# A transformer-layer kernel: ten adding DMAs sent at other weight units, cross-output differences kept in PSUM, two row turns moved together, one weight split put later

## The chip, the cores and the metric

The kernel runs on one core of one Trainium2 chip. The metric is the device time of one execution in microseconds (us). TensorE multiplies matrices (PE in the profile, its weight loads PEld), VectorE (DVE) and ScalarE (ACT) do elementwise work, GpSimd (POOL) does small elementwise work and issues DMAs of its own, and SyncE (SP) issues most of the weight loads.

## The reference

One layer of a bidirectional encoder on 512 tokens of width 1024, in float32. It has three sub-layers, and each is added to the residual after a norm:

```python
h = rmsnorm(x, pre_mix_g)                                  # 1. token mixing
aq, ak, av, hq, hf_fwd, hf_bwd, hi, hg = split_columns(h @ w_in, IN_SPLITS)
att = axial_gqa_attention(rope(norm(aq)), rope(norm(ak)), av)
rec = hgrn2_group(hq, hf_fwd, hf_bwd, hi, hg, lb, hg_out_norm_g)
x = x + rmsnorm(concat([att, rec]) @ w_out, post_mix_g)
h = rmsnorm(x, pre_x_g); m = rmsnorm(mem, mem_norm_g)      # 2. cross-attention, 256 memory rows
x = x + rmsnorm(memory_cross_attention(h, m, w_xq, w_xkv, w_xo), post_x_g)
h = rmsnorm(x, pre_ffn_g)                                  # 3. gated MLP
u = depthwise_conv3(h @ w_up) + conv_b                     # 2 x 2816 columns
gate, val = split(u, 2)
x = x + rmsnorm((silu(gate) * val) @ w_down, post_ffn_g)
```

## The kernel before

**Products.** Every large product is made of three matmuls on float32r halves: an operand is split into a high part (a cast, on ScalarE) and a low part (the difference, on VectorE), and `mm3` (lines 323 to 325) adds high times high, high times low and low times high in a PSUM bank. PSUM has eight banks of 128 x 512, two for each of the four tags "b", "s", "c" and "o"; a new tile of a tag waits until the oldest of its two is released by its last reader.

**Weight units.** Weights come in units of 128 x 1024 (512 KB). SP loads a unit into a `raw` buffer (line 229; two of them), `issue` casts it to `wh` on ScalarE (line 267) and subtracts to `wl` on VectorE (line 269). For some units the low part is made otherwise: ScalarE or GpSimd writes -wh (lines 274, 272) and a DMA of GpSimd's queue adds the weights to it in flight (line 275). A unit is issued three ahead of its use. Units 38 to 45 are the mixing output projection, 46 to 49 the memory values, 50 to 57 the queries, 58 to 71 the cross output, and from 72 (`N_UP`) on the up-projection.

**Weight sums.** The down-projection uses sums of weight blocks (the Strassen-Winograd scheme: seven products in place of eight). They are made in DRAM by DMAs alone: a *seed* copies a first block to `sum_t` (line 293, SP's queue, after units 28 to 45 and 60 to 65), and later an *add* adds the second block to it in flight (line 296, GpSimd's queue). There are 24 adds, in a fixed order; the set `adds_at` names the units after which one goes out. Ten of its entries are `ADDS_AT`, the others are units of the up-projection. GpSimd first copies one column of the unit's `wl` to `mark` (line 281), so that the add follows that unit's low part. Every sixth add is half as large.

**Mixing output and queries.** `res_second` takes units 42 to 45 for the second half of the output columns, row block by row block. For each block of 128 rows the output is squared and summed on ScalarE (line 377), GpSimd makes the inverse root (lines 348, 351), VectorE multiplies by the gain (379) and adds to x (384), ScalarE squares again (401), VectorE scales (355), TensorE turns the rows (line 362), and ScalarE and VectorE split the turned rows (151, 152). The queries (units 50 to 57) then multiply them; `put_qx` splits each product (lines 1094, 1095). Meanwhile SP loads the eight half blocks of the cross output weights (line 1106) and VectorE adds them in place (line 1111).

**Cross output.** The output of the cross-attention is again seven products in place of eight, with running sums in PSUM: `near_y` (tag "c"), `far_y` ("s") and `last_y` ("b"). Four small steps take a difference or a sum with a kept product: `far_near` (line 1205), `far_far` (1210), `near_far` (1215) and `near_done` (1228); each writes a tile in SBUF, which the norm of that half row block then squares and multiplies. Row blocks 2 and 3 ("far") are turned while the last products run (`OUT_TURN`). Row blocks 0 and 1 ("near") are turned in the up-projection.

**Start of the up-projection.** Its first four products (`us`, banks b, s, c, o) run first on the far 256 columns, then on the near 256. `UP_TURN` names the product n of the first part after which a near row block is turned: (1, 2) turns block 0 after product 1 and block 1 after product 2.

**What sets the order.** The order of instructions on each engine is fixed when the program is built, by a scheduler that follows the order of the code and its own estimate of times. `tc.issue_after(ins)` puts the block's instructions behind `ins` on the engine of `ins`.

Of the kernel before, what the change touches and what calls it, by code (L numbers as in the profile page):

```python
# [28 lines left out]
UP_S = (6, 8, 9, 11, 12, 14, 15, 17, 18, 20)  # L29
N_PLAIN, N_MIX, N_WHOLE = 58, 66, 110 - 2 * len(UP_S)  # L30
N_UP = N_PLAIN + 14
# [11 lines left out]
SIDES_AT = (19, 20)  # L43
LOW_FROM = {"diag": 0, "last": 512}
SEEDS_AT = frozenset(range(28, 46)) | frozenset(range(60, 66))
ADDS_AT = frozenset(range(45, 65, 2))
XO_LOADS = {1: [('w11', 0), ('w11', 1)], 2: [('w12', 0), ('w12', 1)], 3: [('w22', 0), ('w22', 1)], 4: [('w21', 0), ('w21', 1)]}
XO_AT = {"w11": 58, "w21": 60, "w12": 62, "w22": 64}
XO_FROM = {"t1": "w11", "t3": "w12", "t4": "w21", "t2": "w22"}
# [5 lines left out]
NEG_GROUP = frozenset((p, 1) for p in (2, 5, 6))  # L55
AHEAD = 3
HOLD_BLOCK = 4
TURN_STEP, MEM_TURN, UP_TURN = 0, (0, 4), (1, 2)
NEG_SCALAR = frozenset(range(9, 33))
NEG_POOL = frozenset(range(33, 42))  # L60
CORE_SHARE, ATT_LEAD = 53.0, 4.0
# [58 lines left out]
def layer(tc, io, out):  # L120
    nc = tc.nc
# [16 lines left out]
    def bank(tag):  # L138
        return ps.tile([P, 512], F32, name="ps_" + tag, tag=tag)
# [4 lines left out]
    def tmp2(shape=(P, 512), dt=F32, tag="ta"):  # L144
        return t2.tile(list(shape), dt, name="tmp2", tag=tag, bufs=TMP_BUFS[tag])

    def tmp4(shape, dt=F32):
        return t4.tile(shape, dt, name="tmp4", tag="tmp4")

    def split(hi, lo, src, eng=None):  # L150
        nc.scalar.copy(hi, src)  # L151
        (eng or nc.vector).tensor_sub(lo, src, hi.bitcast(F32))  # L152

    def split_scaled(hi, lo, src, factor):
# [22 lines left out]
    for i, name in enumerate(XO_UNITS):  # L177
# [4 lines left out]
            plan.append(("w", XO_AT[name] + u) if name in XO_AT else ("xs", (name, u)))  # L182
        if name in XO_BY_DMA:
            by_adding.add(N_PLAIN + i)
    whole, adds_at = N_MIX, set(ADDS_AT)
    for i in range(NF):
        if i in UP_S:
            plan += [(kind, UP_S.index(i)) for kind in ("diag", "side", "sums", "last")]
        else:
            if i >= 2:  # L190
                adds_at.update((len(plan), len(plan) + (i - 1 not in UP_S)))
            plan += [("w", whole), ("w", whole + 1)]
            whole += 2
    assert len(plan) == N_DOWN and whole == N_WHOLE
# [50 lines left out]
    def issue():  # L245
        i = issued[0]
        issued[0] += 1
        raw = raws.popleft() if raws else load_w()
        kind = plan[i][0] if i < N_DOWN else "w"
        if kind == "diag" and not raws:  # L250
            raws.append(load_w())
        if kind in ("side", "sums", "last"):
            raw = pair_sums[kind]
        elif kind == "xs":
            name, u = plan[i][1]
            raw = cross_blocks[XO_FROM[name]][:, u, :]
        if kind == "keep":
            kept = big([P, 2, 1024], F32R)
            wh, wl = kept[:, 0], kept[:, 1]
        else:  # L260
            wh = wp.tile([P, 1024], F32R, name="wh", tag="wh")
            wl = wp.tile([P, 1024], F32R, name="wl", tag="wl")
        if raw.shape[1] < 1024:
            wh, wl = wh[:, :raw.shape[1]], wl[:, :raw.shape[1]]
        next_to = kind == "diag" and plan[i - 4][0] == "diag"
        by_dma = 1024 if next_to else 0 if i in by_adding or i in NEG_POOL else LOW_FROM.get(kind, raw.shape[1])
        nc.scalar.copy(wh, raw)  # L267
        if by_dma:
            last_low[0] = nc.vector.tensor_sub(wl[:, :by_dma], raw[:, :by_dma], wh[:, :by_dma].bitcast(F32)).ins  # L269
        if by_dma < raw.shape[1]:  # L270
            if i in NEG_POOL:
                nc.gpsimd.tensor_scalar(wl, wh.bitcast(F32), -1.0, 0.0, op0=ALU.mult, op1=ALU.add)
            else:
                nc.scalar.mul(wl[:, by_dma:], wh[:, by_dma:].bitcast(F32), -1.0)  # L274
            nc.gpsimd.dma_start(wl[:, by_dma:], source(i)[:, by_dma:], accum_op=ALU.add)  # L275
        add_blocks(kind, raw, raws[0] if raws else None)
        pending.append((wh, wl))
        if i in SEEDS_AT:
            seeds.popleft()()
        if i in adds_at and adds:  # L280
            with tc.issue_after(nc.gpsimd.tensor_copy(mark, wl[:, 0:1].bitcast(F32)).ins):
                adds.popleft()()

    seeds, adds = deque(), deque()

# [916 lines left out]
    c21 = [tmp2(tag="tq") for _ in range(2)]  # L1202

    def far_near(b):
        nc.vector.tensor_sub(c21[b], c21[b], far_y[b])
        got[2 + b] = first_part(2 + b, c21[b])

    def far_far(b):
        c22 = tmp2(tag="tq")
        nc.vector.tensor_sub(c22, far_y[b], kept[:, 2 + b])  # L1210
        turns.append(second_part(2 + b, got[2 + b], c22))

    def near_far(b):
        c12 = tmp2(tag="tq")
        nc.vector.tensor_sub(c12, far_y[b], kept[:, b])
        got[b] = first_part(b, c12, 1)

    drain(cross_product(near_y, "a22", 1, unit(2), False, True, True, lambda b: nc.scalar.copy(c21[b], near_y[b])))
    drain(cross_product(far_y, "r2", 1, unit(2), False, True, False, far_near))
# [4 lines left out]
    far_done = last_mm[0]  # L1224
    hi, lo = left["a12"]
    def near_done(b):
        c11 = tmp2(tag="tq")
        nc.vector.tensor_add(c11, last_y[b], kept[:, b])
        return second_part(b, got[b], c11, 0, True)

    for b in range(2):
        for i in range(2):
# [76 lines left out]
    for part in range(2):  # L1309
        cols = half_t[1 - part]  # L1310
        for n in range(4):
            for kc in range(8):
                mm3(us[n][:, cols], (ws[n][0][:, kc, :], ws[n][1][:, kc, :]), hT.get(kc, cols), kc == 0, kc == 7)
            if part:
                conv(*first[n], us[n])
            elif n in UP_TURN:
                turns.popleft()()
    fulls = [big([P, 4, T]) for _ in range(2)]
    wide = [big([P, 2, 4, 256]) for _ in range(2)]
    s1, s2, s3, s4 = wide[0][:, 0], wide[0][:, 1], wide[1][:, 0], wide[1][:, 1]  # L1320
# [243 lines left out]
```

## Time and profile before

| | before |
|---|---|
| median of 3 runs | 813.32 us (813.09 to 813.73) |
| the profiled execution | 813.2 us, span 811.4 us |
| TensorE busy | 794.7 us (98%) |
| VectorE, ScalarE, GpSimd busy | 615.1, 515.7, 155.3 us |
| SP's queue (q1), GpSimd's queue (q0) | 36.0% and 29.3% of 16 DMA engines' span |
| weight loads `raw<-in_w_dram` on SP | 75, median 4.4 us from issue to landing |
| adds `sum_t<-in_wd_dram`, `sum_t<-sum_t` on GpSimd | 10 and 10 of 512 KB, median 7.9 and 8.6 us |

The span is the time from the first to the last instruction in the profile; the execution's own time is 1.8 us more. A row of the timeline has its start in us from the span's start, its length, engine, line, operation, the tile it writes and those it reads, and in brackets how long the engine had been idle and what ended the wait. A row of a windows view has, for each engine, the busy time in a stretch and the number of instructions, then the granted clock, the busy share of the DMA engines and GB/s. A row of waits has who waited for whom, the total in us, how many times, and the longest.

### The profile page before, as it was taken

The numbers are of one execution on the slowest core, as the hardware profiler recorded it, in microseconds if no ns is written. First come the engines' busy times: TensorE is split into PE (matmuls) and PEld (weight loads), VectorE is DVE, ScalarE is ACT, GpSimd is POOL, SyncE is SP. The second block draws the span as 40 slices with busy tenths as digits, with TensorE's granted clock in tenths as the row PEclk, the third lists the DMA queues.
The fourth block names the chain that finished last, engine by engine and source line by source line (L and its number), as shares of the span: only waits on it lengthen the run. The fifth ranks groups of instructions, "written<-read, shape, count | busy, mean of one in ns | idle before, by whom it ended". The sixth has DMA issues, their size and how long they took to land.

```text
span 811.4 us, 12058 instructions
## 1 busy us (share of the span) xinstructions
PE 794.7 (98%) x4474; PEld 687.2 (85%) x4474; DVE 615.1 (76%) x945; ACT 515.7 (64%) x860; POOL 155.3 (19%) x221
## 2 busy tenths in 40 slices
PE   9999999999999999999999999999999999999996
PEld 7888888899988888877888898899999999888884
DVE  5466586698796865748478859877897897998775
ACT  6675774678988864544676845556665664767651
POOL 0111201324223102401001621210210121010301
PEclk9999999999999999999999999999999999999998
DMA  8597666669878754497934839663764666378842
GB/s 302 193 265 169 134 151 131 143 178 275 225 180 197 188 197 120 113 257 265 287 64 134 212 105 255 143 157 96 202 163 121 169 168 170 100 234 285 240 116 103
DMA packets 44476, 146.19 MB, mean 180 GB/s; under 512 B 5505, under 2 KB 6785, under 8 KB 44417
## 3 DMA queue, kind: packets, MB, share of 16 engines
q1 hardware_dynamic: 29808, 100.58, 36.0%
q0 software_dynamic: 13312, 41.95, 29.3%
q10 hardware_dynamic: 1296, 2.89, 0.9%
q8 instruction: 35, 0.57, 0.3%
q14 instruction: 25, 0.20, 0.1%
HBM read 141.73 MB, written 25.17 MB: 206 GB/s over the span
## 4 chain that ended last, share of the span: by engine, by line
PE 81%; DVE 6%; ACT 5%; DMA 4%; POOL 2%; issue 2%; SPq 0%; DVEq 0%; POOLq 0%; ACTq 0%
PE ps_b L324 8%; PE ps_b L323 8%; PE ps_b L325 8%; PE ps_s L323 6%; PE ps_s L325 6%; PE ps_s L324 6%; PE ps_o L323 5%; PE ps_o L324 5%; PE ps_o L325 5%; PE ps_c L323 4%; PE ps_c L325 4%; PE ps_c L324 4%; DMA raw<-in_w_dram 4%; PE ps_c L726 2%; PE ps_o L989 2%
## 5 line engine op out<-in xcount | busy, mean ns | idle before, releaser
L267 ACT CAST wh<-raw 128x1024 fp32r<-128x1024 f32 x104 | 107.5, 1036 | 79.2 <-PE ps_b L324 21.2
L323 PE MATMUL ps_b<-big,wh 128*128 128x512 f32 (+1 forms) x364 | 129.2, 355 | 1.2 <-ACT big L151 1.1
L324 PE MATMUL ps_b<-big,wh 128*128 128x512 f32 (+1 forms) x364 | 127.5, 350 | 1.3 <-DVE big L152 1.3
L325 PE MATMUL ps_b<-big,wl 128*128 128x512 f32 (+1 forms) x364 | 127.2, 349 | 0.0
L269 DVE TENSOR_TENSOR wl<-raw,wh 128x1024 fp32r<-128x1024 f32 (+1 forms) x61 | 70.1, 1154 | 37.0 <-ACT wh L267 36.9
L323 PEld LDWEIGHTS ps_b<-big,wh 128*128 128x128 f32 x364 | 68.9, 189 | 10.6 <-ACT big L151 2.0
L324 PEld LDWEIGHTS ps_b<-big,wh 128*128 128x128 f32 x364 | 68.9, 189 | 10.1 <-DVE big L152 1.8
L325 PEld LDWEIGHTS ps_b<-big,wl 128*128 128x128 f32 x364 | 68.8, 189 | 9.0
L275 POOL DMA_DIRECT2D wl<-in_w_dram x39 | 35.1, 901 | 126.6 <-ACT wl L274 109.0
L323 PE MATMUL ps_s<-wh,big 128*128 128x512 f32 (+1 forms) x148 | 56.8, 385 | 0.1
L324 PE MATMUL ps_s<-wl,big 128*128 128x512 f32 (+1 forms) x148 | 56.2, 380 | 0.0
L325 PE MATMUL ps_s<-wh,big 128*128 128x512 f32 (+1 forms) x148 | 56.1, 379 | 0.0
L755 DVE TENSOR_TENSOR big<-big 128x512 f32<-128x512 f32 x64 | 47.6, 760 | 8.4 <-PE ps_c L726 3.5
L323 PE MATMUL ps_s<-big,wh 128*128 128x256 f32 (+1 forms) x160 | 47.9, 299 | 0.0
L325 PE MATMUL ps_s<-big,wl 128*128 128x256 f32 (+1 forms) x160 | 47.8, 299 | 0.0
L324 PE MATMUL ps_s<-big,wh 128*128 128x256 f32 (+1 forms) x160 | 47.8, 299 | 0.0
L274 ACT ACTIVATE wl<-wh 128x1024 fp32r<-128x1024 f32 (+1 forms) x46 | 44.3, 962 | 0.6
L152 DVE TENSOR_TENSOR big<-ps_o,big 128x512 fp32r<-128x512 f32 (+1 forms) x55 | 36.3, 666 | 9.0 <-ACT big L151 7.0
L267 ACT CAST wh<-big 128x1024 fp32r<-128x1024 f32 (+1 forms) x28 | 28.2, 1008 | 19.4 <-PE ps_c L325 5.6
L275 POOL DMA_DIRECT2D wl<-in_wu_dram x16 | 13.9, 869 | 133.7 <-ACT tmp L1360 120.1
L269 DVE TENSOR_TENSOR wl<-big,wh 128x1024 fp32r<-128x1024 f32 (+1 forms) x28 | 32.3, 1162 | 9.3 <-ACT wh L267 7.5
L348 POOL TENSOR_SCALAR small<-small 128x1 f32<-128x1 f32 x40 | 18.9, 473 | 87.7 <-ACT tmp L1396 40.4
(342 smaller groups left out, 2271.3 us busy)
## 6 DMA issues: line engine op xcount, KB each, us to landing
raw<-in_w_dram SPq DMA_DIRECT2D x75, 512.0 KB, 4.4
wl<-in_w_dram POOLq DMA_DIRECT2D x39, 512.0 KB, 6.5
sum_t<-in_wd_dram SPq DMA_DIRECT2D x20, 512.0 KB, 6.9
tmp<-in_w_dram SPq DMA_DIRECT2D x12, 512.0 KB, 4.9
raw<-in_wu_dram SPq DMA_DIRECT2D x12, 512.0 KB, 4.1
sum_t<-in_wd_dram POOLq DMA_DIRECT2D x10, 512.0 KB, 7.9
sum_t<-sum_t POOLq DMA_DIRECT2D x10, 512.0 KB, 8.6
big<-sum_t SPq DMA_DIRECT2D x10, 512.0 KB, 4.4
```

Source lines behind the costliest of these rows:

```text
L152: (eng or nc.vector).tensor_sub(lo, src, hi.bitcast(F32))
L267: nc.scalar.copy(wh, raw)
L269: last_low[0] = nc.vector.tensor_sub(wl[:, :by_dma], raw[:, :by_dma], wh[:, :by_dma].bitcast(F32)).ins
L274: nc.scalar.mul(wl[:, by_dma:], wh[:, by_dma:].bitcast(F32), -1.0)
L275: nc.gpsimd.dma_start(wl[:, by_dma:], source(i)[:, by_dma:], accum_op=ALU.add)
L323: nc.tensor.matmul(o, a[0], b[0], start=start, stop=False, skip_group_check=again)
L324: nc.tensor.matmul(o, a[0], b[1], start=False, stop=False, skip_group_check=again)
L325: last_mm[0] = nc.tensor.matmul(o, a[1], b[0], start=False, stop=stop, skip_group_check=again).ins
L348: nc.gpsimd.tensor_scalar(ss[:, i + 4:i + 5], ss[:, i:i + 1], 1.0 / D, ss[:, i + 3:i + 4] if i else EPS, op0=ALU.mult, op1=ALU.add)
L726: nc.tensor.matmul(o[:, b, :], kc[:, blk(b)], qc[:, blk(b)] if m == 1 else pat(qk, b * P, [[2 * m, P // (2 * m)], [T + m, 2], [1, m]]), st ...
L755: nc.vector.tensor_tensor(out=c, in0=c, in1=pat(tt, toff + off, [[2, npair], [gap, 2], [0, m]]), op=ALU.mult)
L989: nc.tensor.matmul(o, vv[:, c, h // 4].rearrange("p a d -> p (a d)"), pt[j][:, c, :], start=c + j == 0, stop=c == 3 and j == 1)
```

## The change

The ten entries of `ADDS_AT` become units 42, 43, 44 (twice), 45 (twice), 59, 60, 61 and 63, in place of 45, 47, ... 63; `adds_at` is a list now, and a unit sends as many adds as it stands there. `far_near` writes into `near_y`, `far_far` into a bank of tag "o", `near_far` and `near_done` in place, all in PSUM. `UP_TURN` becomes (2, 2): both near row blocks are turned after product 2. The cast of unit `N_UP` + 3 (75) is put on ScalarE behind the last cast that `split` has made by then, that of the last turned far rows.

```diff
--- before.py
+++ after.py
@@ -43,7 +43,7 @@
 SIDES_AT = (19, 20)
 LOW_FROM = {"diag": 0, "last": 512}
 SEEDS_AT = frozenset(range(28, 46)) | frozenset(range(60, 66))
-ADDS_AT = frozenset(range(45, 65, 2))
+ADDS_AT = (42, 43, 44, 44, 45, 45, 59, 60, 61, 63)
 XO_LOADS = {1: [('w11', 0), ('w11', 1)], 2: [('w12', 0), ('w12', 1)], 3: [('w22', 0), ('w22', 1)], 4: [('w21', 0), ('w21', 1)]}
 XO_AT = {"w11": 58, "w21": 60, "w12": 62, "w22": 64}
 XO_FROM = {"t1": "w11", "t3": "w12", "t4": "w21", "t2": "w22"}
@@ -55,7 +55,7 @@
 NEG_GROUP = frozenset((p, 1) for p in (2, 5, 6))
 AHEAD = 3
 HOLD_BLOCK = 4
-TURN_STEP, MEM_TURN, UP_TURN = 0, (0, 4), (1, 2)
+TURN_STEP, MEM_TURN, UP_TURN = 0, (0, 4), (2, 2)
 NEG_SCALAR = frozenset(range(9, 33))
 NEG_POOL = frozenset(range(33, 42))
 CORE_SHARE, ATT_LEAD = 53.0, 4.0
@@ -147,8 +147,10 @@
     def tmp4(shape, dt=F32):
         return t4.tile(shape, dt, name="tmp4", tag="tmp4")
 
+    last_high = [None]
+
     def split(hi, lo, src, eng=None):
-        nc.scalar.copy(hi, src)
+        last_high[0] = nc.scalar.copy(hi, src).ins
         (eng or nc.vector).tensor_sub(lo, src, hi.bitcast(F32))
 
     def split_scaled(hi, lo, src, factor):
@@ -182,13 +184,13 @@
             plan.append(("w", XO_AT[name] + u) if name in XO_AT else ("xs", (name, u)))
         if name in XO_BY_DMA:
             by_adding.add(N_PLAIN + i)
-    whole, adds_at = N_MIX, set(ADDS_AT)
+    whole, adds_at = N_MIX, list(ADDS_AT)
     for i in range(NF):
         if i in UP_S:
             plan += [(kind, UP_S.index(i)) for kind in ("diag", "side", "sums", "last")]
         else:
             if i >= 2:
-                adds_at.update((len(plan), len(plan) + (i - 1 not in UP_S)))
+                adds_at += sorted({len(plan), len(plan) + (i - 1 not in UP_S)})
             plan += [("w", whole), ("w", whole + 1)]
             whole += 2
     assert len(plan) == N_DOWN and whole == N_WHOLE
@@ -264,7 +266,11 @@
             wh, wl = wh[:, :raw.shape[1]], wl[:, :raw.shape[1]]
         next_to = kind == "diag" and plan[i - 4][0] == "diag"
         by_dma = 1024 if next_to else 0 if i in by_adding or i in NEG_POOL else LOW_FROM.get(kind, raw.shape[1])
-        nc.scalar.copy(wh, raw)
+        if i == N_UP + 3:
+            with tc.issue_after(last_high[0]):
+                nc.scalar.copy(wh, raw)
+        else:
+            nc.scalar.copy(wh, raw)
         if by_dma:
             last_low[0] = nc.vector.tensor_sub(wl[:, :by_dma], raw[:, :by_dma], wh[:, :by_dma].bitcast(F32)).ins
         if by_dma < raw.shape[1]:
@@ -279,7 +285,8 @@
             seeds.popleft()()
         if i in adds_at and adds:
             with tc.issue_after(nc.gpsimd.tensor_copy(mark, wl[:, 0:1].bitcast(F32)).ins):
-                adds.popleft()()
+                for _ in range(min(len(adds), adds_at.count(i))):
+                    adds.popleft()()
 
     seeds, adds = deque(), deque()
 
@@ -1202,18 +1209,17 @@
     c21 = [tmp2(tag="tq") for _ in range(2)]
 
     def far_near(b):
-        nc.vector.tensor_sub(c21[b], c21[b], far_y[b])
-        got[2 + b] = first_part(2 + b, c21[b])
+        nc.vector.tensor_sub(near_y[b], c21[b], far_y[b])
+        got[2 + b] = first_part(2 + b, near_y[b])
 
     def far_far(b):
-        c22 = tmp2(tag="tq")
+        c22 = bank("o")
         nc.vector.tensor_sub(c22, far_y[b], kept[:, 2 + b])
         turns.append(second_part(2 + b, got[2 + b], c22))
 
     def near_far(b):
-        c12 = tmp2(tag="tq")
-        nc.vector.tensor_sub(c12, far_y[b], kept[:, b])
-        got[b] = first_part(b, c12, 1)
+        nc.vector.tensor_sub(far_y[b], far_y[b], kept[:, b])
+        got[b] = first_part(b, far_y[b], 1)
 
     drain(cross_product(near_y, "a22", 1, unit(2), False, True, True, lambda b: nc.scalar.copy(c21[b], near_y[b])))
     drain(cross_product(far_y, "r2", 1, unit(2), False, True, False, far_near))
@@ -1224,9 +1230,8 @@
     far_done = last_mm[0]
     hi, lo = left["a12"]
     def near_done(b):
-        c11 = tmp2(tag="tq")
-        nc.vector.tensor_add(c11, last_y[b], kept[:, b])
-        return second_part(b, got[b], c11, 0, True)
+        nc.vector.tensor_add(last_y[b], last_y[b], kept[:, b])
+        return second_part(b, got[b], last_y[b], 0, True)
 
     for b in range(2):
         for i in range(2):
@@ -1313,8 +1318,9 @@
                 mm3(us[n][:, cols], (ws[n][0][:, kc, :], ws[n][1][:, kc, :]), hT.get(kc, cols), kc == 0, kc == 7)
             if part:
                 conv(*first[n], us[n])
-            elif n in UP_TURN:
-                turns.popleft()()
+            else:
+                for _ in range(UP_TURN.count(n)):
+                    turns.popleft()()
     fulls = [big([P, 4, T]) for _ in range(2)]
     wide = [big([P, 2, 4, 256]) for _ in range(2)]
     s1, s2, s3, s4 = wide[0][:, 0], wide[0][:, 1], wide[1][:, 0], wide[1][:, 1]
```

## The prediction

> **What bounds the kernel now.** I read the page's first lines, then the waits of TensorE, then the windows, and only then the timeline around each wait.
>
> ```profile
> span 811.4 us, 12058 instructions
> PE 794.7 (98%) x4474; PEld 687.2 (85%) x4474; DVE 615.1 (76%) x945; ACT 515.7 (64%) x860; POOL 155.3 (19%) x221
> PE ps_s L325 <- DVE big L1095: 1.6, 1, 1.6
> PE ps_b L362 <- DVE tmp L355: 1.4, 1, 1.4
> PE ps_b L324 <- DVE big L152: 1.3, 2, 0.9
> 296.00:308.00 12.00, 12.00 (x60) 9.66 (x59) 5.28 (x10) 6.08 (x11) 1.10 (x2) 1.00 0.95 335
> 345.00:385.00 40.00, 37.06 (x188) 30.88 (x186) 26.83 (x32) 17.47 (x29) 5.20 (x9) 1.00 0.85 261
> 440.00:475.00 35.00, 32.51 (x193) 27.71 (x192) 27.62 (x41) 24.47 (x50) 17.93 (x28) 1.00 0.66 166
> ```
>
> TensorE is busy for 98% of the span, and the change leaves its matmuls as they are. So only its idle time can be won, 16.7 us in all. The waits and windows say where: 2.9 us in 345 to 385 (query projection) and 2.5 us in 440 to 475 (cross output and start of the up-projection). The granted clock is 1.00 in each window, so the throttle plays no part. The profiled execution took 813.2 us, 1.8 over its span; the median of the runs, 813.3, is 0.1 above it. I sum against 813.2.
>
> **Part 1: six adding transfers leave the query stage.** Before, the adds go out after units 45, 47, ... 63; unit 45 is the last of the output projection, 46 to 49 are the memory values, 50 to 57 the queries. After, the first six go out at 42, 43, 44, 44, 45, 45 and four at 59, 60, 61, 63.
>
> ```profile
> raw<-in_w_dram SPq DMA_DIRECT2D x1, 512.0 KB, 3.3
> raw<-in_w_dram SPq DMA_DIRECT2D x1, 512.0 KB, 6.1
> q0 software_dynamic: 135, 0.49, 47.6%
> q1 hardware_dynamic: 187, 0.70, 41.2%
> 345.36 0.39 PE L324 MATMUL ps_s<-wl,big 128*128 128x512 f32 x1
> 345.59 0.39 PE L325 MATMUL ps_s<-wh,big 128*128 128x512 f32 x1
> 344.86 1.05 ACT L267 CAST wh<-raw 128x1024 fp32r<-128x1024 f32 x1 [5.20 <-DMA raw<-in_w_dram]
> 345.82 0.58 ACT L151 CAST big<-ps_c 128x512 fp32r<-128x512 f32 x1
> 348.16 0.40 PE L325 MATMUL ps_b<-big,wl 128*128 128x512 f32 x1
> ```
>
> The first two rows are weight loads on SP's queue: the one issued at 331.3 landed in 3.3 us, with no add about; the one issued at 338.64, with the add of unit 47 (issued 336.11) in flight, took 6.1. The queue rows are those of 338.6 to 344.8: q0, POOL's, held 47.6% of 6.2 us of the 16 engines, 2.95 us, nearly all of one add. So an add costs a load beside it about 2.9 us. That load was unit 50's. ScalarE stood 5.20 us at its cast, with the two casts of the last turned rows queued behind it (345.82), and TensorE needed those. Three matmul steps, 345.59 to 348.16, took 2.57 us in place of three times 0.23: **gap A, 1.9 us**. Without the adds of 47 and 49 the load lands at 341.9, the casts end at 344.0, their differences at 345.5, before TensorE asks at 345.8. I take all 1.9 (between 1.0 and 1.9).
>
> ```profile
> 380.44 0.39 PE L325 MATMUL ps_s<-big 128*128 128x256 f32 x1 [1.59 <-DVE big L1095]
> 378.56 1.22 DVE L1111 TENSOR_TENSOR big<-big 128x1024 f32<-128x1024 f32 x1
> 379.70 0.68 DVE L1095 SCALAR_TENSOR_TENSOR big<-ps_b,big 128x512 fp32r<-128x512 f32 x1
> raw<-in_w_dram SPq DMA_DIRECT2D x1, 512.0 KB, 11.8
> sum_t<-in_wd_dram POOLq DMA_DIRECT2D x1, 512.0 KB, 9.9
> ```
>
> **Gap B**, 1.6 us: the fourth query's low part, L1095, stood on VectorE behind a block sum, L1111. VectorE had a backlog because loads issued at 357 took 11.8 us beside an add of 9.9. Three adds (51, 53, 55) go from this stretch, some 2.9 us each, so loads come more than 4 us sooner while TensorE comes 1.9 sooner. The order of VectorE's queue may still put an L1111 ahead; the cast that L1095 waits for follows TensorE itself, so 0.3 or so stays. I take 1.3, all but about a fifth (0 to 1.6). Sum of part 1: -3.2.
>
> **Part 2: what the same adds cost where they go.**
>
> ```profile
> 303.93 0.33 SPq L229 DMA_DIRECT2D raw<-in_w_dram  x1
> raw<-in_w_dram SPq DMA_DIRECT2D x1, 512.0 KB, 5.5
> 311.59 1.06 ACT L267 CAST wh<-raw 128x1024 fp32r<-128x1024 f32 x1
> 312.68 1.23 DVE L269 TENSOR_TENSOR wl<-raw,wh 128x1024 fp32r<-128x1024 f32 x1 [0.35 <-ACT wh L267]
> 313.96 0.19 PEld L324 LDWEIGHTS ps_s<-wl,big 128*128 128x128 f32 x1 [0.38 <-DVE wl L269]
> raw<-in_w_dram SPq DMA_DIRECT2D x1, 512.0 KB, 3.2
> sum_t<-in_wd_dram POOLq DMA_DIRECT2D x1, 512.0 KB, 8.1
> q0 software_dynamic: 198, 0.75, 68.6%
> q1 hardware_dynamic: 194, 0.73, 34.6%
> ```
>
> Unit 45's load, issued at 303.93, stands in SP's queue behind the four rows of x and lands at 309.4. Its cast follows at 311.59, and TensorE already waits 0.38 us for its low part: 2.2 us of slack, then every us counts. DMA is 0.95 busy from 296 to 308 (row above). The add of unit 43 displaces 2.95 us there, less 0.6 idle: landing 311.7, a stall of 0.2. The two adds of unit 44 follow its difference at about 304.2 and 305. Where both queues are full they alternate (387 to 393, last two rows: 198 against 194 packets) and the adds get two thirds of the time. If they start at once after the gains, the load crawls at a third of the rate to about 316.7, a stall of 5.2. Against that, unit 46's load (313.93) had an add issued 0.3 us after it and still landed in 3.2 (the pair 3.2 and 8.1). That is the nearest row in order of issue, though without a queue ahead. So 0.2 to 5.2, taken nearer the low end: **+1.9**. A stall here shifts everything after it; nothing later gives it back.
>
> [...]
>
> POOL itself: a mark copy and a DMA issue of 0.8 to 0.9 us each. Behind 42 and 43 stand the two gains (297.93), behind 44's two the first row sums (310.50); behind 45's two, which end near 315.9, one at 316.31. None is passed. At 59 to 63 the transfers run where no weight load is due (none is issued from 391 to 419): 0, bounds -0.3 and +0.5. SP issues what it did.
>
> **Part 3: cross output, turns and the split of unit 75.**
>
> ```profile
> 459.01 1.05 ACT L267 CAST wh<-raw 128x1024 fp32r<-128x1024 f32 x1
> 461.77 0.68 DVE L152 TENSOR_TENSOR big<-ps_o,big 128x512 fp32r<-128x512 f32 x1
> 462.37 0.68 DVE L379 TENSOR_TENSOR tmp<-tmp,big 128x512 f32<-128x512 f32 x1
> 461.91 0.39 PE L324 MATMUL ps_b<-big,wh 128*128 128x256 f32 x1 [0.45 <-DVE big L152]
> 463.74 0.92 POOL L275 DMA_DIRECT2D wl<-in_w_dram  x1
> 469.15 0.66 PE L362 MATMUL ps_b<-ident,tmp 128*128 128x128 f32 x4 [1.35 <-DVE tmp L355]
> 473.18 0.62 PE L362 MATMUL ps_c<-ident,tmp 128*128 128x128 f32 x4
> 474.16 0.36 PE L323 MATMUL ps_o<-big,wh 128*128 128x256 f32 x1
> ```
>
> The cast of unit 75 (459.01) ran between the casts of the last far rows and cost ScalarE 0.95 us there; it now follows them. But VectorE does its four L152 back to back until 462.4, so the up-projection, which waits for their low parts, gains nothing from that alone. And there is a new wait: the first up product takes a bank "b", and both are last_y's. Before, L1228 freed one at 459.4; now last_y itself is squared and multiplied, so it is free after L379, at 462.4 to 463.05. The first product starts 0.6 to 1.2 us later than at 461.8.
>
> The turn of row 0 no longer stops TensorE at 467.6 (1.5 us until 469.15): three products of 2.88 run first, to about 471.3, and row 0 is ready by then. The two turns take 2.0 and end near 473.3 in place of 474.16: **-0.85**, if row 1 is ready by 472.3. It was ready at 473.1, with POOL's issue for unit 75 (463.74) just ahead of its row sum; unit 75's moved chain and ScalarE's 0.95 should give that 0.6 to 0.8. Bounds: -1.8 (row 1 early, bank free early) and +0.7 (row 1 no earlier, bank late). Unit 75's low part landed at 469.1 and is used at 474: 5 us of cover; moved by 2 us it costs nothing, moved by more than 5 each us counts. The differences written to PSUM are the same VectorE instructions, 0.68 us; the multiply L379 reads PSUM in the output projection at the same price:
>
> ```profile
> 316.16 0.69 DVE L379 TENSOR_TENSOR tmp<-ps_s,big 128x512 f32<-128x512 f32 x1 [1.66 <-ACT tmp L377]
> ```
>
> [...]
>
> **Sum.** 813.2 - 1.9 - 1.3 + 1.9 - 0.85 = 811.05; with the 0.1 to the median, 811.2.
>
> **The rivals.**
> No stall at unit 45: the adds of 44 start as late as the one at 357 (issued 357.43, landing in 9.9). For it speaks the pair 3.2 and 8.1. Then 811.2 - 1.9 = 809.3.
> The other side, slower: the adds of 44 take the engines from unit 45's load at once. The place is the weight load at 313.96, the price up to 5.2, and it decides from a stall of 4.05, where the gains are used up (load landing after 315.5). It gives 811.2 + 3.3 = 814.5. For it speaks the alternation in 387 to 393; against it unit 46's load.
> VectorE's order stays, so B stays, with the load in between: 811.2 + 1.3 = 812.5.
> Turning rows 0 and 1 later only moves the wait to row 1, as 473.18 suggests: 811.2 + 0.85 = 812.05.
>
> **How the numbers follow.** A measurement of this kernel tells about 0.2%, 1.6 us, from no change: faster is below 811.7. The forecast (810.2 to 812.2) 0.40, of it 0.29 faster; no stall 0.20, all faster; full stall 0.17, of it 0.12 slower; B stays 0.13, of it 0.01 faster and 0.01 slower; row 1 waits 0.10, of it 0.02 faster. Faster 0.52, same 0.35, slower 0.13. The range, 809.0 to 814.0, leaves out a tenth on each side: the low end is the no-stall case with 0.3 more, the high end stops short of the full stall. The forecast's own range is 810.2 to 812.2.
>
> **What would show it.** Part 1: loads of units 50 to 56 in 3 to 6 us, no wait of 5 us before unit 50's cast, TensorE's waits for L151/L152 at its first query and for L1095 gone or under 0.5. Part 2: a longer wait for unit 45's L269 near 314. Part 3: the first up product waits for L379 rather than L152, and no wait before row 0's turn. The prediction is wrong if unit 45 stalls over 4 us, or if B's wait stays whole.

## The result, and the profile after

| | before | after |
|---|---|---|
| median | 813.53 us (813.09 to 815.03, 4 runs) | 805.99 us (805.41 to 806.37, 4 runs) |
| ratio after to before | | 0.9903, 95% interval 0.9886 to 0.9921 |
| the profiled execution | 813.2 us, span 811.4 | 806.27 us, span 804.5 |

The change made the kernel 0.97% faster. The forecast was 811.2 with a range of 809.0 to 814.0: the direction was right, the size was not, and the time lies 3 us below the range.

The first lines of the page of after, then its windows over two of the stretches that the prediction argued about:

```profile
span 804.5 us, 12059 instructions
PE 793.2 (99%) x4474; PEld 688.1 (86%) x4474; DVE 615.0 (76%) x945; ACT 515.9 (64%) x860; POOL 151.7 (19%) x219
```

```profile
345.00:385.00 40.00, 40.00 (x204) 34.20 (x203) 27.36 (x36) 20.26 (x40) 0.95 (x1) 1.00 0.74 262
440.00:475.00 35.00, 34.28 (x232) 31.33 (x232) 25.50 (x39) 22.61 (x48) 15.64 (x27) 1.00 0.66 176
```

(Line numbers move by 2 to 7: L229 is L231 now, L267 is L273, L152 is L154, L324 is L331, L355 is L362, L362 is L369, L379 is L386, L384 is L391, L1095 is L1102, L1228 is L1233; unit 75's cast has L271. In the runs with part of the edits the numbers lie between.) In the query stretch, 345 to 385, TensorE is never idle, where it had stood 2.94 us. In 440 to 475 it stands 0.72 in place of 2.49, in one wait for a low part (the row at 456.72 below). The three waits that headed the list of before (L1095, L355, L152 twice) are gone but for that.

Both kernels issue 4474 matmuls, so I can follow the same matmul, counted in order of start from zero, through both traces. That gives the time between two counts, free of what happened earlier:

| | 1920 to 1960: gap A | 1960 to 2160: gap B | 2160 to 2440 | 2440 to 2600: cross output, turns | start of 1920 |
|---|---|---|---|---|---|
| before | 10.98 | 41.02 | 56.85 | 25.65 | 343.10 |
| after | 9.07 | 38.93 | 56.85 | 22.92 | 342.74 |
| difference | -1.91 | -2.09 | 0 | -2.73 | -0.36 |

The sum is 7.09; behind matmul 2600 after takes 0.16 more, which leaves the 6.93 by which the spans differ. The 0.36 up to 343 isn't the change's: 0.45 was there at matmul 1000 (187 us), ahead of the first moved add (282 us), and from 1000 to 1920, beside the moved adds, after takes 0.09 more (155.40 against 155.31). Other executions of these kernels had from -0.6 to +1.5 at 1920 (the last column of the table further down).

**The stall that did not come.** The prediction charged 1.9 us (0.2 to 5.2) near 314. The timeline of SP and ScalarE in after, and the DMA view for the load issued at 303.48:

```profile
303.48 0.33 SPq L231 DMA_DIRECT2D raw<-in_w_dram  x1
...
311.23 1.05 ACT L273 CAST wh<-raw 128x1024 fp32r<-128x1024 f32 x1
328.02 1.05 ACT L273 CAST wh<-raw 128x1024 fp32r<-128x1024 f32 x1 [0.68 <-PE ps_o L332]
```

```profile
raw<-in_w_dram SPq DMA_DIRECT2D x1, 512.0 KB, 12.0
```

The load did get late, about as the prediction worked out: 12.0 us in place of 5.5, landing at 315.5. But the cast at 311.23 began 4.3 us before it landed, and waited for nothing. So it casts another load. The next cast is at 328.02, and it waited for a matmul. The load had 12.5 us to spare.

**Gap A.** ScalarE's cast of unit 50 and the last of its turned rows, then TensorE at its first query:

```profile
341.65 1.05 ACT L273 CAST wh<-raw 128x1024 fp32r<-128x1024 f32 x1 [2.23 <-DMA raw<-in_w_dram]
342.61 0.58 ACT L153 CAST big<-ps_c 128x512 fp32r<-128x512 f32 x1
345.68 0.39 PE L331 MATMUL ps_b<-big,wh 128*128 128x512 f32 x1
345.91 0.39 PE L332 MATMUL ps_b<-big,wl 128*128 128x512 f32 x1
```

The wait before unit 50's cast is 2.23 in place of 5.20, the cast of the turned row is 3.2 us sooner (342.61 against 345.82), and the first matmuls follow each other at 0.23. The second one shown is the one that began at 348.16 in before.

**Gap B.** VectorE and TensorE at the fourth query:

```profile
371.25 1.22 DVE L1118 TENSOR_TENSOR big<-big 128x1024 f32<-128x1024 f32 x1
372.39 0.68 DVE L1102 SCALAR_TENSOR_TENSOR big<-ps_b,big 128x512 fp32r<-128x512 f32 x1
376.17 0.28 PE L332 MATMUL ps_s<-big 128*128 128x256 f32 x1
```

The low part L1102 still stands right behind a block sum, but it ends at 373.1, 3.1 us before the matmul that had waited for it in before (376.17; by count the same as that at 380.44).

**Cross output.** VectorE's and TensorE's rows at the start of the up-projection and at the turns:

```profile
455.39 0.69 DVE L1233 TENSOR_TENSOR ps_b<-ps_b,big 128x512 f32<-128x512 f32 x1
455.72 0.28 PE L330 MATMUL ps_s<-big,wh 128*128 128x256 f32 x1
455.99 0.68 DVE L154 TENSOR_TENSOR big<-ps_c,big 128x512 fp32r<-128x512 f32 x1
456.72 0.39 PE L331 MATMUL ps_s<-big,wh 128*128 128x256 f32 x1 [0.72 <-DVE big L154]
465.18 1.42 DVE L362 SCALAR_TENSOR_TENSOR tmp<-big,small 128x512 f32<-128x512 f32 x2 [0.80 <-POOL small L358]
465.34 0.60 PE L369 MATMUL ps_b<-ident,tmp 128*128 128x128 f32 x4
466.21 0.60 PE L369 MATMUL ps_c<-ident,tmp 128*128 128x128 f32 x4
```

TensorE takes its first up product in a bank "s" (455.72), not "b". So it does in every run with the PSUM writes, and in every run without them "b" comes first. It waits once there, 0.72. At 465.34 both turns follow without a wait. Row 1's second half (L362) ends at 466.60; the turn that reads it begins at 466.65, the next one after 466.21. It is ready with next to nothing to spare.

### The profile page after: what moved, and what is told of

It reads as the page before. It is cut to its first block, busy times and chain, and to the rows that moved or that the text cites. A ratio compares the mean times of both kernels' runs of the same rounds, so it can differ in the third digit from the quotient of the medians.

```text
span 804.5 us, 12059 instructions
## 1 busy us (share of the span) xinstructions
PE 793.2 (99%) x4474; PEld 688.1 (86%) x4474; DVE 615.0 (76%) x945; ACT 515.9 (64%) x860; POOL 151.7 (19%) x219
## 4 chain that ended last, share of the span: by engine, by line
PE 89%; DVE 5%; ACT 3%; issue 1%; POOL 1%; DMA 0%; DVEq 0%; POOLq 0%; ACTq 0%
PE ps_b L331 9%; PE ps_b L330 9%; PE ps_b L332 9%; PE ps_s L330 7%; PE ps_s L331 7%; PE ps_s L332 7%; PE ps_o L330 5%; PE ps_o L331 5%; PE ps_o L332 5%; PE ps_c L330 4%; PE ps_c L331 4%; PE ps_c L332 4%; PE ps_c L733 2%; PE ps_o L996 2%; PE ps_s L564 1%; PE ps_o L564 1%
## 5 line engine op out<-in xcount | busy, mean ns | idle before, releaser
L273 ACT CAST wh<-raw 128x1024 fp32r<-128x1024 f32 (+1 forms) x103 | 106.6, 1036 | 72.6 <-PE ps_b L331 26.3
L331 PE MATMUL ps_b<-big,wh 128*128 128x512 f32 (+1 forms) x364 | 127.3, 350 | 0.0
L331 PEld LDWEIGHTS ps_b<-big,wh 128*128 128x128 f32 x364 | 68.9, 189 | 8.2
L331 PE MATMUL ps_s<-wl,big 128*128 128x512 f32 (+1 forms) x148 | 56.3, 380 | 0.0
L331 PE MATMUL ps_s<-big,wh 128*128 128x256 f32 (+1 forms) x160 | 47.9, 299 | 0.7 <-DVE big L154 0.7
L154 DVE TENSOR_TENSOR big<-ps_o,big 128x512 fp32r<-128x512 f32 (+1 forms) x55 | 36.3, 666 | 8.1 <-ACT big L153 6.0
L273 ACT CAST wh<-big 128x1024 fp32r<-128x1024 f32 (+1 forms) x28 | 28.2, 1007 | 20.5 <-PE ps_c L332 5.6
L153 ACT CAST big<-ps_o 128x512 fp32r<-128x512 f32 (+1 forms) x55 | 31.5, 574 | 5.8 <-PE ps_o L985 2.9
```

The costliest lines, as they stand in the source:

```text
L153: last_high[0] = nc.scalar.copy(hi, src).ins
L331: nc.tensor.matmul(o, a[0], b[1], start=False, stop=False, skip_group_check=again)
```

## The experiments

In what follows *after* and *before* stand for the two kernels, a ratio is to the runs of before on the same chip, with its 95% interval, and the stages are those of the table above. The kernels were timed in groups, each beside its own runs of before, whose median was 812.65 to 814.29. After was not timed again beside them, so differences of medians to its 805.99 are rough; the stages are of one profiled execution each.

| kernel | median us | ratio | A | B | cross output | start of 1920 |
|---|---|---|---|---|---|---|
| adds_only | 809.17 | 0.9948 (0.9933 to 0.9963) | 9.07 | 38.93 | 25.98 | 342.58 |
| cross_only | 810.87 | 0.9973 (0.9959 to 0.9988) | 9.85 | 42.76 | 23.73 | 342.56 |
| adds_six_44 | 806.04 | 0.9912 (0.9894 to 0.9931) | 9.07 | 38.93 | 22.65 | 343.53 |
| adds_47_49 | 806.89 | 0.9924 (0.9906 to 0.9943) | 10.39 | 38.92 | 22.66 | 342.47 |
| adds_51_55 | 806.93 | 0.9920 (0.9903 to 0.9937) | 9.07 | 39.55 | 22.91 | 342.80 |
| no_psum | 808.63 | 0.9938 (0.9924 to 0.9953) | 9.07 | 38.93 | 25.43 | 342.78 |
| no_turn | 807.81 | 0.9933 (0.9917 to 0.9949) | 9.07 | 38.93 | 25.41 | 344.52 |
| no_turn_again (one run) | 809.22 | | 9.07 | 38.93 | 24.07 | 344.55 |
| no_split | 807.88 | 0.9931 (0.9915 to 0.9948) | 9.07 | 38.93 | 24.86 | 343.07 |
| adds_psum | 808.22 | 0.9948 (0.9936 to 0.9961) | 9.07 | 38.92 | 24.88 | 342.81 |
| adds_turn | 809.33 | 0.9962 (0.9949 to 0.9974) | 9.07 | 38.93 | 25.93 | 343.04 |
| adds_split | 808.67 | 0.9952 (0.9940 to 0.9964) | 9.07 | 38.93 | 25.42 | 342.88 |
| late_add | 806.69 | 0.9930 (0.9917 to 0.9944) | 9.07 | 38.93 | 23.20 | 342.90 |

### The adds alone

```diff
 before, with
-ADDS_AT = frozenset(range(45, 65, 2))
+ADDS_AT = (42, 43, 44, 44, 45, 45, 59, 60, 61, 63)
```

> The kernel before with only the list of adding transfers of after (42, 43, 44, 44, 45, 45, 59, 60, 61, 63). Theory: the query stage gives the 1.9 us before its first product (gap A) and the 2.1 us by its fourth (gap B) that the trace of after shows, and nothing is lost near 314, since the load issued at 303.9 beside these adds is unit 46's and is cast only at 328: 809.2 to 809.6, with no wait over 0.5 us of TensorE near 314. Rival 1, the prediction as recorded: a stall of 1.9 near 314 and B of 1.3, so 812.2. Rival 2: part of the 2.1 at gap B comes only through the later edits, since they change the order of all engines' work: 810.0 to 810.5. In each case 2.7 us of the change stay out, at 459 to 477.

809.17: the theory held (0.03 under its range). A and B are those of after to the hundredth, and nothing is lost near 314: from matmul 1000 to 1920 it takes 155.24, before 155.31. Its waits of TensorE in 440 to 475:

```profile
PE ps_b L363 <- DVE tmp L356: 1.3, 1, 1.3
PE ps_b L324 <- ACT big L151: 0.7, 1, 0.7
PE ps_b L325 <- DVE big L152: 0.5, 1, 0.5
```

These are the waits of before in that stretch, 2.59 us idle against 2.49. So the two halves of the change are separate: the adds bring 4.0 us in the query stage, the rest lies in the cross output.

### The cross output's edits alone

```diff
 before, with the differences in PSUM, UP_TURN = (2, 2) and unit 75's cast behind the turned rows'
 ADDS_AT = frozenset(range(45, 65, 2))
```

> The kernel before with only the edits of the cross output, the turns and unit 75's split; the ten adding transfers stay at 45, 47, ... 63. Theory: these edits alone bring the 2.7 us that TensorE gained between 459 and 477 in after, whatever the adds do: 810.6 to 811.0, with the wait of 1.35 us before row 0's turn gone and the first up product in a bank s rather than b. Rival 1, the prediction as recorded: 0.85 us, 812.7, the first up product waiting 0.6 to 1.2 us for a bank b. Rival 2: the gain needs the earlier queries, because VectorE arrives at the cross output with less behind it; then under 1.5 us, above 812.0.

810.87 lies in the theory's range, but not by its mechanism. The cross output's stage took 23.73, 1.92 less than before, not 2.73: a wait of 0.9 for a low part made by DMA had come in. Gap A took 1.1 less than before by itself, since unit 50's load, beside the same add, happened to take 5.0 us where before's took 6.1. And gap B took 1.7 more. The two waits of TensorE, then the windows at the first of them, then a window of before at the same place:

```profile
PE ps_s L331 <- DVE big L1101: 1.6, 1, 1.6
...
PE ps_s L331 <- DMA wl<-in_w_dram: 0.9, 1, 0.9
```

```profile
377.07:378.94 1.87, 0.28 (x2) 0.08 (x2) 1.87 (x4) 1.87 (x3) 0.00 (x0) 1.00 0.02 7
378.94:380.60 1.66, 1.66 (x8) 1.66 (x9) 1.66 (x2) 1.27 (x2) 0.00 (x0) 0.52 0.01 5
380.60:382.30 1.70, 1.70 (x8) 1.51 (x8) 1.70 (x3) 0.00 (x0) 1.02 (x2) 0.50 0.08 10
```

```profile
380.60:384.00 3.40, 3.40 (x24) 3.14 (x25) 3.40 (x4) 1.09 (x2) 1.22 (x2) 1.00 0.15 27
```

The third number from the end is the granted clock. The wait is the same 1.6 us as in before, but behind it the clock was 0.52 and 0.50 for 3.4 us (in before 1.00). That is the 1.7 us.

### All six early adds beside one load

```diff
-ADDS_AT = (42, 43, 44, 44, 45, 45, 59, 60, 61, 63)
+ADDS_AT = (44, 44, 44, 44, 44, 44, 59, 60, 61, 63)
```

> The kernel after with the six early adds all sent behind unit 44's difference (44 six times, then 59, 60, 61, 63). Six adds of some 2.95 us of the engines each are 17.7 us of transfers from 304 on. Theory: the load beside them is unit 46's, wanted only at 328, so it may land as late as 324 to 326 and TensorE loses nothing: within 0.6 us of after (805.6 to 806.6); unit 47's load, issued near 314, lands late too but is wanted near 333. Rival, the prediction's reading: the load issued at 303.9 is wanted at 311.6, and each add in front of it costs TensorE about 2.9 us: 5 to 12 us over after, 811 to 818.

806.04, ratio 0.9912 against 0.9903 of after: nothing lost. The DMA view for the load at 304.33 and for the last (half) add, and ScalarE's cast:

```profile
raw<-in_w_dram SPq DMA_DIRECT2D x1, 512.0 KB, 5.0
...
sum_t<-in_wd_dram POOLq DMA_DIRECT2D x1, 256.0 KB, 17.6
```

```profile
328.82 1.05 ACT L273 CAST wh<-raw 128x1024 fp32r<-128x1024 f32 x1 [0.68 <-PE ps_o L332]
```

The theory's number for the load was wrong: it landed in 5.0 us, at 309.3; the adds, issued from 0.3 us behind it on, took until 324.9, and the next load, issued at 314.39 behind all six, took 7.9. So this run shows that six adds there cost nothing; whose load it is it can't tell, as 309.3 would have served a cast at 312 as well. That is told by after itself, where the load landed at 315.5, behind the cast of 311.23.

### Adds put back to 47 and 49, or to 51, 53 and 55

```diff
 adds_47_49: ADDS_AT = (42, 43, 44, 44, 47, 49, 59, 60, 61, 63)
 adds_51_55: ADDS_AT = (42, 43, 44, 51, 53, 55, 59, 60, 61, 63)
```

> The kernel after with two of the early adds put back to where the kernel before had them, units 47 and 49 (42, 43, 44, 44, 47, 49, 59, 60, 61, 63). Theory: gap A alone comes back, because unit 50's load shares the engines with these adds and lands some 2.9 us later, and the two casts of turned rows stand behind unit 50's cast: +1.5 to +2.1 over after, 807.5 to 808.1, with a wait of about 5 us before unit 50's cast; gap B stays gone, as loads from 351 on have no add beside them. Rival: A was the product of five adds together (the queue of loads behind), and two alone cost less than 0.6 us.

> The kernel after with three of the early adds put back to units 51, 53 and 55 (42, 43, 44, 51, 53, 55, 59, 60, 61, 63). Theory: gap A stays gone, since unit 50's load has no add beside it, and gap B comes back, since the loads from 357 on crawl beside adds, VectorE gets its backlog and L1101 stands behind a block sum again: +1.6 to +2.1 over after, 807.4 to 808.1, more in executions where the clock dips behind that wait as it did in the run with the cross edits alone (1.6 more). Rival: the backlog at B came from the lateness at A, not from the adds of 51 to 55 themselves; then under 0.5 over after.

Each brings back its own gap and leaves the other alone, but smaller than expected: A +1.32, B +0.62; 806.89 and 806.93, under both ranges. First adds_47_49 at the first query, then adds_51_55 at the fourth:

```profile
343.64 1.05 ACT L273 CAST wh<-raw 128x1024 fp32r<-128x1024 f32 x1 [4.65 <-DMA raw<-in_w_dram]
346.60 0.50 PE L331 MATMUL ps_b<-big,wh 128*128 128x512 f32 x1 [0.87 <-DVE big L154]
```

```profile
376.01 0.68 DVE L1102 SCALAR_TENSOR_TENSOR big<-ps_b,big 128x512 fp32r<-128x512 f32 x1
376.75 0.39 PE L332 MATMUL ps_s<-big 128*128 128x256 f32 x1 [0.36 <-DVE big L1102]
```

Gap A follows the load of unit 50: it took 6.1 us in before and cost 1.9, 5.5 in adds_47_49 and cost 1.3, 5.0 in cross_only and cost 0.8, 3.3 in after and cost nothing. Between 5.0 and 6.1 us, each us of that load was about one us of TensorE. Gap B is a queue on VectorE. Counted from matmul 1960, TensorE comes to the step that reads the fourth low part after 24.4 us. The low part ended at 21.3 in after, 22.0 in adds_47_49, 24.8 in adds_51_55 and 26.3 in before, and the stage lost 0, 0, 0.62 and 2.09. So the three adds do most of the delaying, but the first 3.1 us of it are covered. The lateness at A alone does not make B: adds_47_49 has the one without the other.

### One of the cross output's edits taken out of after

```diff
 no_psum: far_near, far_far, near_far and near_done write tmp2 tiles in SBUF, as before
 no_turn: UP_TURN = (1, 2), as before
 no_split: unit 75's cast without issue_after, as before
```

> The kernel after with the four differences of the cross output written to SBUF as before; adds, turns and split as after. Theory 1: the PSUM writes carry the gain at the first up product, because without the ring of tmp2 buffers VectorE and ScalarE need not wait for a buffer there and the order written around 455 changes: +0.7 to +1.5, 806.7 to 807.5. Theory 2: they carry nothing, being the same VectorE work, and the gain is that of the turns and the split: within 0.4 of after (805.6 to 806.4). The prediction as recorded had them cost 0.6 to 1.2 by a late bank b: then this run would be 0.6 or more under after.

> The kernel after with row 0 turned behind up product 1 and row 1 behind 2, as before. Theory: TensorE waits again before row 0's turn, as it did for 1.35 us in the kernel before and in the run with the earlier adds alone: +1.0 to +1.6, 807.0 to 807.6. Rival: with unit 75's chain out of the way row 0 is ready in time (in after its difference ended near 463, the products before it near 462), so the turn's place no longer matters: under 0.5.

> The kernel after with unit 75's cast left in its place among the casts of the last far rows. Theory: ScalarE's 1.05 us of that cast comes back ahead of the last casts, so the low parts that the first up product waits for are late by that: +0.6 to +1.2, 806.6 to 807.2, with the wait before the first product's L154 near 1.5. Rival, the prediction as recorded: VectorE does its four low parts back to back and is the later one, so the split alone changes nothing at the first product: within 0.3 of after.

By the medians all three lie above their ranges, 2.6, 1.8 and 1.9 us over after. By the stage no_turn does not: 1.15 (below). The first profile of no_turn does not show its place: TensorE waited 0.8 for a low part made by DMA, and then the clock fell, as the window tells:

```profile
461.00:462.00 1.00, 1.00 (x6) 1.00 (x6) 1.00 (x2) 0.56 (x2) 0.42 (x2) 0.50 0.82 209
```

So it has a second execution with a profile:

> The kernel after with row 0 turned behind product 1 and row 1 behind 2, in a second execution with a profile: in the first one the clock fell and a transfer was late between 459 and 464, so that the place of the loss was covered. Theory: without these, TensorE waits 1.5 to 2 before row 0's turn (it comes near 462.5, the row is ready near 464.4), and nothing before row 1's: 807.5 to 807.9. Rival: row 0's turn does not wait and the time is lost at the first up product.

The waits of TensorE in 440 to 475, of no_psum, of no_split and of no_turn_again:

```profile
PE ps_b L330 <- ACT big L153: 0.8, 1, 0.8
PE ps_c L369 <- DVE tmp L362: 0.8, 1, 0.8
PE ps_b L331 <- DVE big L154: 0.7, 1, 0.7
```

```profile
PE ps_c L363 <- DVE tmp L356: 1.0, 1, 1.0
PE ps_s L324 <- ACT big L151: 0.9, 1, 0.9
PE ps_s L325 <- DVE big L152: 0.2, 1, 0.2
```

```profile
PE ps_b L369 <- DVE tmp L362: 0.9, 1, 0.9
PE ps_s L331 <- DVE big L154: 0.7, 1, 0.7
```

In the stage no_psum costs 2.51, no_split 1.94 and no_turn_again 1.15 us. Without the PSUM writes or without the split, the first product waits twice (L153 and L154; in no_split these are L151 and L152) and row 1's turn, in bank "c", waits too. Without the later turn the first product does as in after, and row 0's turn, in bank "b", waits 0.9, less than the 1.5 to 2 expected. Its one time of 809.22 has 1.8 us in it that were lost before 343; five of the six runs of no_turn lie at 807.46 to 807.86.

### One edit on top of the adds

```diff
 adds_only, with the PSUM writes, or UP_TURN = (2, 2), or unit 75's cast behind the turned rows'
```

> The kernel before with the moved adds and the PSUM writes; turns and unit 75's split as before. Taking any one of the three edits out of after cost 1.8 to 2.6 of the 2.7 us that all three bring. Theory: they work only together (the chain from the last far rows to row 1's turn has no slack in after, 466.60 against 466.65), so one alone gives at most 0.7 over the adds alone: 808.4 to 809.3. Rival: each edit has a share of its own, and the PSUM writes the largest (no_psum lost the most): 807.0 to 808.0.

> The kernel before with the moved adds and the two turns behind product 2. Theory of edits that work only together: 808.4 to 809.3, row 0's wait of 1.3 gone and a wait of 0.8 to 1.5 before row 1's turn in its place. The prediction as recorded, for its rows: the turns end 0.85 sooner through this edit together with the split, so 808.3 at the best. Rival: the turn alone brings the whole wait of 1.5: 807.5 to 807.9.

> The kernel before with the moved adds and unit 75's cast behind the last far rows' casts. Theory of edits that work only together: 808.4 to 809.3, since row 0's turn stays behind product 1, where its wait takes whatever the first product gains. The prediction as recorded says nothing is gained at the first product, as VectorE's four low parts end the wait: 809.0 to 809.3. Rival: ScalarE's 1.05 us shows at the first product in full: 807.9 to 808.2.

Against adds_only's 25.98 the stage takes (24.07 is that of no_turn_again, whose clock did not fall):

| | neither PSUM nor split | PSUM | split | PSUM and split |
|---|---|---|---|---|
| turn as before | 25.98 | 24.88 | 25.42 | 24.07 |
| turn later | 25.93 | 24.86 | 25.43 | 22.92 |

The PSUM writes bring 1.1, the split 0.6, both 1.9. The later turn brings nothing unless both are there, and then 1.15. "Only together" held for the turn and not for the PSUM writes (808.22, 0.2 under the range). The split alone brings 0.56, which that theory's bound of 0.7 allows, so its range (808.67 lies in it) does not decide. The wait that shows why, in adds_turn:

```profile
PE ps_c L363 <- DVE tmp L356: 1.6, 1, 1.6
```

In adds_only row 0's turn (bank "b") waits 1.3. With the later turn that wait is gone and row 1's (bank "c") is 1.6. The PSUM writes and the split make row 1 ready sooner; with either alone it is still late, with both it is ready at 466.60.

When the second half of row 1 has been scaled, counted from matmul 2440, says more than the stage: 22.08 us in adds_only, 20.98 with the PSUM writes, 21.52 with the split, 18.99 with both (no_turn_again). Both together bring 3.1, 1.4 more than the two shares of 1.1 and 0.6. VectorE's order shows where the 1.4 comes from. First adds_psum, then after:

```profile
463.27 1.41 DVE L356 SCALAR_TENSOR_TENSOR tmp<-big,small 128x512 f32<-128x512 f32 x2 [1.07 <-POOL small L352]
464.60 0.74 DVE L385 SCALAR_TENSOR_TENSOR big<-tmp,small,big 128x512 f32<-128x512 f32 x1
```

```profile
461.11 1.42 DVE L391 SCALAR_TENSOR_TENSOR big<-tmp,small,big 128x512 f32<-128x512 f32 x2 [0.73 <-POOL small L358]
462.97 1.41 DVE L362 SCALAR_TENSOR_TENSOR tmp<-big,small 128x512 f32<-128x512 f32 x2 [0.44 <-POOL small L358]
```

Without both edits, the second addition of row 1 to x (L385 at 464.60; L391 in after) stands behind the two scalings of row 0; so it does with neither, with either alone and in before. With both, the two additions come ahead of row 0's scalings.

### The remaining wait of after

```diff
 def near_done(b):
-    nc.vector.tensor_add(last_y[b], last_y[b], kept[:, b])
+    with tc.issue_after(last_split[0]):
+        nc.vector.tensor_add(last_y[b], last_y[b], kept[:, b])
```

> The kernel after with both additions of the near rows (L1233) held until the last low part of the far rows' turn. In after one of them stands on VectorE between these low parts, and TensorE's first up product waits 0.72 for a low part. Theory: the first product starts 0.6 sooner, but row 1's turn, which in after is ready just when TensorE comes (difference ends 466.60, last half of the turn starts 466.65), now makes it wait: between 0.3 faster than after and 0.5 slower, 805.7 to 806.5. Rival: row 1 moves up with its products: 0.6 faster, 805.4.

```profile
PE ps_c L369 <- DVE tmp L362: 0.3, 1, 0.3
```

The wait at the first product is gone from the list, and row 1's turn waits in its place. The stage takes 23.20, 0.28 more than in after; 806.69. The theory's mechanism held, though the first product gains only 0.3 and not 0.6; its range missed by 0.2 us. By the medians after stays the fastest of these kernels, but adds_six_44 (806.04) can't be told from it, and the intervals of the ratios of late_add and of several others overlap with that of after.

## Why the prediction was wrong

**Part 1, gap A: right.** -1.9 forecast, -1.91 measured, by the chain that was named: unit 50's load lands at 341.6 (341.9 forecast), its cast lets the casts of the turned rows go, and TensorE does not stop. adds_47_49 brings it back. The hit to the hundredth is luck: with the same add beside the same load, cross_only lost 0.8 and adds_47_49 1.3 where before lost 1.9.

**Part 1, gap B: right, too small.** -1.3 (0 to 1.6) forecast, -2.09 measured. Of the wait "0.3 or so stays", I wrote, because the cast ahead of L1095 follows TensorE. None stays: L1102 ends 3.1 us early, because VectorE's whole queue is ahead. I also took the wait's column (1.6) for its cost. From start to start that step is 1.87 in before (378.57 to 380.44) where its neighbours take 0.12, so it cost 1.75, and of the rest 0.24 was lost just ahead of it, between the matmuls 2060 and 2080.

**Part 2: the step that failed first.** "Unit 45's load, issued at 303.93 ... Its cast follows at 311.59 ... 2.2 us of slack". There are two raw buffers, so a load may go out when the unit *two* ahead of it has been split. The load that goes out at the end of unit 44's split is unit 46's. After shows which split that is: unit 44's two adds are issued at 304.10 and 304.66, just behind it. Unit 45's own load had gone out at 293.67 in before and landed in 3.2 us. I had taken the next cast in time for the next load's. (The load at 313.93, which I called unit 46's, is unit 47's for the same reason.) The arithmetic on the transfer itself was fair (315.5 measured; 311.7 to 316.7 forecast), the chain behind it was that of another unit, and with it the whole +1.9, the rival at 814.5 and the upper half of the range fell. The case "no stall" (0.20) came out, but not for its reason: the load did get late, landing at 315.5, where my own chain had all the slack used up and a stall of 4.05. It took 12.0 us, and the two adds of unit 44 beside it 9.3 and 11.5.

**Part 3: right in direction, a third of the size.** -0.85 (-1.8 to +0.7) forecast, -2.73 measured. Two steps failed.
- "there is a new wait: the first up product takes a bank 'b' ... starts 0.6 to 1.2 us later". I read the order of the products from before and held it fixed. The scheduler took the product in bank "s" first, and the one in "b" second. The second matmul of the first product, at 461.91 in before, is at 456.72: 5.2 us sooner, of which 4.4 were gained ahead of it, so 0.8 sooner and not 0.6 to 1.2 later. no_psum, in which the product in "b" is first again, has both waits back.
- Row 1: "unit 75's moved chain and ScalarE's 0.95 should give that 0.6 to 0.8". I let the stage end 0.85 sooner because I took row 1 to become the limit at 472.3. The 473.1 is the end of its first half; its second ended at 473.69 in before and at 466.60 in after, 7.1 us sooner, of which 4.4 were gained ahead of it and 2.7 here. The runs with one edit show where that comes from: the PSUM writes (1.1, costed at nothing, as "the same VectorE instructions"), the split (0.6), and the order on VectorE that only both bring (1.4).

What makes the PSUM writes worth 1.1 us can be read from the traces, though no run tries it by itself. The VectorE instructions are as long as before (L1233 0.69, L386 0.68), so it is not their duration. Nor is it the order: the 1.1 is there already when a far row is scaled (2.71 us after matmul 2440 in adds_only, 1.57 in adds_psum), and until then VectorE, ScalarE and GpSimd work in the same order in both. The difference is on GpSimd, which makes the inverse root. First adds_only, then adds_psum:

```profile
443.69 0.68 DVE L380 TENSOR_TENSOR tmp<-tmp,big 128x512 f32<-128x512 f32 x1
443.73 0.78 POOL L349 TENSOR_SCALAR small<-small 128x1 f32<-128x1 f32 x1 [3.26 <-ACT tmp L378]
```

```profile
443.91 0.68 DVE L380 TENSOR_TENSOR tmp<-ps_o,big 128x512 f32<-128x512 f32 x1
443.86 0.26 POOL L349 TENSOR_SCALAR small<-small 128x1 f32<-128x1 f32 x1 [3.18 <-ACT tmp L378]
```

While VectorE multiplied a tile in SBUF, GpSimd's small step took 0.78 and ended 0.13 behind it; while VectorE multiplied a tile in PSUM, it took 0.26. Counted from matmul 2440, VectorE's next step (L385) follows 0.6 sooner. At the next row the same comes again (1.39 against 0.86; in before at 449.98 and after at 445.39, 1.44 against 0.86), and that makes 1.1.

**The sum.** 811.2 forecast, 805.99 measured: 1.9 from the stall that did not come, 0.8 from B, 1.9 from part 3, 0.4 of the start of that execution, and 0.3 between it and the median. Without the stall the same sum gives 809.3, still inside the range; it is part 3 and B, both too small, that put the time below 809.0.

## What to carry to other kernels

Before a late transfer is charged to a consumer, count buffers: with n buffers, the load that goes out when a unit is done belongs to the unit n further on, and the next use in time is that of an earlier load (here n is 2, and the load issued at 303.48 in after was cast at 328.02). Where several edits shorten one chain with two waits in it, cost the chain and not the edits: here moving the first wait away brought nothing by itself (25.93 against 25.98 us) until what the second waits for was ready (22.92 against 24.07). And an order that a scheduler makes from the program is not kept by the change, so a wait that exists only in the old order is a rival and not a term. Last, compare the small steps of the engine beside it, too: VectorE's multiply was 0.68 us long both times, and GpSimd's step took 0.78 us beside the one from SBUF and 0.26 beside the one from PSUM.

## What the runs showed of the hardware

- **The clock after a short stop.** In cross_only TensorE's granted clock was 0.52 and 0.50 for the 3.4 us behind a stop of 1.6 us, and cost 1.7 us. In before the same stop had no such fall (1.00 in 378.9 to 384). In no_turn it fell too, to 0.50 from 461 to 464, behind two stops of 0.7 and 0.8. What decides whether it falls was not tried. The mean clocks of the timed runs go with it, though they do not show the place: 8 of the 35 of before have a mean granted clock of 0.995 and a median of 814.4 us, the 16 with 0.997 have 812.7; of cross_only's nine, three have 0.995; of the 64 runs with early adds moved, none has (the fall in no_turn shows as 0.996).
- **A load and the adds around it.** In adds_six_44 a load issued 0.3 us ahead of six adds took 5.0 us, landing at 309.3, though the last of these landed only at 324.9; the next load, issued behind all six, took 7.9 where that of before took 3.2. In after a load issued 0.6 us ahead of two adds took 12.0. There the rows of x ahead of it were late as well, the last landing at 311.7 in place of 307.3 in before. How much of the 12.0 is theirs was not tried.
- **GpSimd beside VectorE.** In before the first small step of GpSimd's inverse root (L348, 128x1, 40 of them) took 0.18 to 0.27 us in the 16 that overlapped no VectorE instruction with SBUF tiles alone. In the 24 that overlapped one, the median was 0.65, the longest 1.44, and 21 of them ended within 0.14 us behind such an instruction. In after (L355) it is 17 with 0.18 to 0.27, and 23 with a median of 0.63 and a longest of 1.22, of which 20 ended so.
